# Other durations for float32r products in the list scheduler of a three-layer transformer kernel

## The chip, the cores and the metric

One core of a Trainium2 chip runs the whole program in one launch. The metric is the device time of that launch in microseconds (us); lower is better. TensorE (PE below) does the matrix products, VectorE (DVE), ScalarE (ACT) and GpSimd (POOL) work beside it, and SyncE (SP) issues the transfers (DMA).

## The reference, cut to what matters

T = 256 tokens, a model width of 1024, a feed-forward width of 2816, all in float32. Two layers of a first block are followed by one layer of a second block.

```python
for l in range(2):                                   # first block
    h = rmsnorm(x, norm_mix[l])
    aq, ak, av, iq, ik, iw, hq, hf, hi, hg, ga, gb = split(h @ w_in[l])
    y_attn = dsa_attention(rope(norm(aq)), rope(norm(ak)), av, rope(iq), rope(ik), iw)   # 8 heads, top-64 keys
    o = hgrn2_chunked(silu(hq), 1 - exp(log_f), hi, log_f)                               # 4 heads, decay per key
    merged = sigmoid(ga) * (y_attn @ w_proj_attn[l]) + sigmoid(gb) * (rmsnorm(o) * silu(hg) @ w_proj_hgrn[l])
    x = x + merged @ w_out[l]
    g, u = split(rmsnorm(x, norm_ffn[l]) @ w_ffn_in[l])
    x = x + (silu(g) * u) @ w_ffn_out[l]

sh1, sc1, g1, sh2, sc2, g2 = split(silu(c) @ ada_w + ada_b)      # second block
h = rms_norm(x, mix_pre_g) * (1 + sc1) + sh1
q, k, v, f_logit, conv_val, conv_gate = split(h @ w_in)
attn = fox_attention(q, k, v, log_sigmoid(f_logit + b_f))
u = silu(layer_norm(causal_depthwise_conv(conv_val * sigmoid(conv_gate))))
x = x + g1 * rms_norm(concat(attn, u) @ w_o, mix_post_g)
h = rms_norm(x, ffn_pre_g) * (1 + sc2) + sh2
x = x + g2 * rms_norm(swiglu_ffn(h), ffn_post_g)
```

## The kernel before, in words

Every matrix product with a weight is done as three products of rounded parts (the type float32r, F32R in the code): an activation is split into xH (rounded) and xL (the rest), a weight into wH and wL, and PE adds xH·wH, xL·wH and xH·wL in PSUM. A weight comes as a tile `raw` of 128x1024 (512 KB), ACT copies it to `wH` with rounding, and DVE subtracts to get `wL`. `raw` has four buffers, `wH` and `wL` six each. `split_into` (L887) does the same with an activation: ACT writes xH, DVE xL.

The helpers are named for the shape of their products: `pair_mm` has 256 columns (all tokens move past a weight tile), `token_mm`, `out_tm` (L908) and the `go` of `first_tm` (L1332) have 512 (weight columns move past a token half).

The program text writes operations in a readable order, and none of them is issued then. `Recorder.record` notes each with what it reads, writes and depends on, and a duration from `Recorder.cost` (L402). `Recorder.issue` then orders them on a model of the five engines, and only after that does `op.emit` (L400) issue each instruction, for which reason nearly all lines of the profile are L400. The order comes about so:

- the rank of an operation is its own duration and the longest chain of durations and hops behind it; with a bias this is its urgency, and PE's urgencies are rounded down to steps of QUANT = 5000 ns:

```python
op.rank = tail + op.cost + (LOAD_LATENCY if op.engine == "DMA" else 0.0)
op.urgency = op.rank + op.bias
if QUANT and op.engine == "PE":
    op.urgency = op.urgency // QUANT * QUANT
```

- the engine that can start first takes the most urgent of the operations that are ready by then and that find a buffer; among equals the one written first. Each engine runs its queue strictly in that order on the chip.
- the durations therefore act twice, in the ranks and in the model's clock, and through them on all engines.

Places of the program that the prediction speaks of:

- `modulated_tm` (L1524) norms and splits the input of the second block's feed-forward, and calls `first_tm`'s `go` for its first tile. For each token half t and each half of the width it scales (`z`, DVE), transposes four times (PE, into a bank `mm`), applies scale and shift (ACT or DVE, four operations of 128x128), and splits; then come the 24 products of that token half.
- `rstd_of` (L836) norms the convolution at L1680: PE sums squares into one bank of PSUM, DVE takes the reciprocal root in some nine small operations, `spread` (L853) transposes the result into the same bank, and DVE multiplies it in. The output projection `out_tm` (L1689) has four accumulators, side_1767 to side_1770, also banks of the group `side`.
- in a layer of the first block, `attend` (L927) runs a head of attention: logits on PE, the maximum on DVE, exponentials on ACT, the scaling of the probabilities on DVE, transposes and products on PE. The HGRN part (L1195 to L1243) climbs a ladder of levels: `blocks` (L1198) makes products of 32x32 from hk and hq, DVE copies them under a mask into `AC` (`copy_predicated`, L1215), and before each level scales hq and hk by the decay. After five levels the diagonal is copied out of `AC` (L1223).

Of the kernel before, what the change touches and what calls it, by code (L numbers as in the profile page):

```python
# [349 lines left out]
class Recorder:  # L350
# [52 lines left out]
    @staticmethod  # L403
    def cost(engine, method, args, kw, views, outs):
        n = int(np.prod((outs or views)[0].shape[1:]))
        psum = any(v.buf.space == "PSUM" for v in views)
        if engine == "DMA":
            v = (outs or views)[0]
            return max(v.shape[0] * n * 4 / 360.0, 640.0)
        if engine == "PE":  # L410
            if method == "transpose":
                return 109.0
            m = int(np.prod(args[1].shape[1:]))
            if args[1].dtype == F32R:
                return max(n * 0.4265, 109.0)
            cost = max(n, m) * 1.667 + 3.0

            return (cost + 81.0) / 4 if m == 32 else (cost + 53.0) / 2 if m == 64 and n > 64 else cost
        if engine == "S":
            ptr = sum(isinstance(kw.get(k), View) for k in ("bias", "scale"))  # L420
            return (51 if psum else 94) + 0.833 * n + 93 * ptr + (93 if "accum_out" in kw else 0)
        if method in ("max",):
            n = int(np.prod(args[1].shape[1:]))
        fast = not psum and method in ("tensor_copy", "tensor_scalar")
        ptr = sum(isinstance(a, View) for a in args[2:{"tensor_scalar": 4, "scalar_tensor_tensor": 3}.get(method, 2)])
        return (68 if method != "memset" else 7) + n / (1.92 if fast else 0.96) + 61 * ptr

    def issue(self):
# [49 lines left out]
        while len(order) < len(ops):  # L478
# [84 lines left out]
            if e == "PE":  # L563
                while t >= window + WINDOW:
                    warm = busy >= ACTIVE
                    busy, window, left = min(left, WINDOW) * rate, window + WINDOW, max(left - WINDOW, 0.0)
                cost, rate = (cost, 2.4) if warm else (max(2.0 * cost, 214.0), 1.2)
                rate = 0.0 if op.thin else rate
                inside = min(cost, window + WINDOW - t)
                busy, left = busy + inside * rate, cost - inside  # L570
# [1143 lines left out]
```

## Time and profile before

| | |
|---|---|
| median of 3 runs | 1130.52 us (1129.08 to 1131.61) |
| profiled execution, its own time | 1129.97 us |
| its span | 1128.2 us, mean granted clock 0.992 |
| PE busy | 1097.2 us (97%) |
| DVE busy | 857.5 us (76%) |
| ACT busy | 595.5 us (53%) |
| instructions | 22970 |

Instructions of PE are matmuls with their weight loads (PEld) beside them. Busy is the union of the times in which an engine had an instruction running. A wait is idle time with the event that ended it. The profile drops the numbers from the names of buffers; the listings of the order below keep them.

### The profile page before, as it was taken

Reading aid. Unit: us, or ns where it says so; the run is one execution under the profiler, and the core shown is the slowest. Engines: PE = TensorE matmul, PEld = TensorE weight load, DVE = VectorE, ACT = ScalarE, POOL = GpSimd, SP = SyncE. Lnnn points to the kernel's source line nnn. Section 1 sums busy time; section 2 is a strip of 40 time slices with the busy share of each in tenths; the row PEclk is TensorE's granted clock in tenths of the full one; section 3 lists DMA queues with packets and bytes.
Section 4 is the critical chain, followed back from the end, with each engine's and each line's share of the span. In section 5 each row is a group of like instructions: output and inputs, shape, how many; then the busy total and the mean of one; then the engine's idle time right before and its main releaser. Section 6 shows DMA issues by size and latency. Waiting matters only on the chain.

```text
span 1128.2 us, 22970 instructions
## 1 busy us (share of the span) xinstructions
PE 1097.2 (97%) x9388; PEld 1034.5 (92%) x9388; DVE 857.5 (76%) x1590; ACT 595.5 (53%) x905; POOL 7.2 (1%) x16
## 2 busy tenths in 40 slices
PE   6999999999999999999999999999899989999996
PEld 6988999999999999888999999999798578999995
DVE  7999976899966589998676998756879668554554
ACT  6744694644444467446744544444754665443442
POOL 1000000000000000000000000000000000000000
PEclk9999999999999999999999999999999999999998
DMA  7553534689956543643345899655457225556550
GB/s 263 186 180 111 197 123 169 207 314 337 335 190 217 189 154 117 210 146 133 132 172 196 288 346 334 218 201 195 145 176 201 95 76 184 175 186 219 189 169 37
DMA packets 59992, 217.47 MB, mean 193 GB/s; under 512 B 6872, under 2 KB 10096, under 8 KB 56816
## 3 DMA queue, kind: packets, MB, share of 16 engines
q1 hardware_dynamic: 59888, 216.02, 55.8%
q8 instruction: 73, 1.20, 0.4%
q14 instruction: 31, 0.25, 0.1%
HBM read 214.19 MB, written 1.63 MB: 191 GB/s over the span
## 4 chain that ended last, share of the span: by engine, by line
PE 89%; DVE 6%; ACT 3%; issue 1%; DMA 1%; SPq 0%; DVEq 0%; ACTq 0%
PE mm L400 60%; PE side L400 29%; ACT t L400 2%; DVE t L400 1%; DVE b L400 1%; DVE wL L400 1%; DMA raw<-in_W 1%; DVE small L400 1%; ACT wH L400 1%; ACT L604 0%; DVE c L400 0%; DVE xL L400 0%; DVE AC L400 0%; SPq L400 0%; DVE sc L400 0%
## 5 line engine op out<-in xcount | busy, mean ns | idle before, releaser
L400 ACT ACTIVATE wH<-raw 128x1024 fp32r<-128x1024 f32 (+1 forms) x390 | 369.0, 968 | 400.5 <-PE mm L400 221.1
L400 DVE TENSOR_TENSOR wL<-raw,wH 128x1024 fp32r<-128x1024 f32 (+1 forms) x390 | 425.6, 1112 | 151.3 <-ACT wH L400 149.4
L400 PE MATMUL mm<-xH,wH 128*128 128x256 f32 x1760 | 486.8, 279 | 9.2 <-ACT wH L400 9.2
L400 PE MATMUL mm<-xH,wL 128*128 128x256 f32 x1760 | 488.3, 280 | 0.8 <-DVE wL L400 0.8
L400 PE MATMUL mm<-xL,wH 128*128 128x256 f32 x1760 | 488.5, 279 | 0.5 <-DVE xL L400 0.5
L400 PEld LDWEIGHTS mm<-xH,wH 128*128 128x128 f32 x1760 | 330.6, 189 | 11.7 <-ACT wH L400 9.2
L400 PEld LDWEIGHTS mm<-xL,wH 128*128 128x128 f32 x1760 | 331.2, 189 | 3.4 <-issue 0.9
L400 PEld LDWEIGHTS mm<-xH,wL 128*128 128x128 f32 x1760 | 330.8, 189 | 3.5 <-DVE wL L400 1.7
L400 PE MATMUL side<-t,wH 128*128 128x256 f32 x704 | 127.6, 281 | 0.0
L400 PEld LDWEIGHTS side<-t,wH 128*128 128x128 f32 x704 | 108.2, 188 | 0.0
L400 PE MATMUL side<-t,wL 128*128 128x256 f32 x352 | 98.8, 281 | 0.0
L400 ACT ACTIVATE t<-t 128x512 f32<-128x512 f32 (+2 forms) x80 | 48.9, 620 | 39.8 <-DVE t L400 37.0
L400 PEld LDWEIGHTS side<-t,wL 128*128 128x128 f32 x352 | 66.2, 188 | 0.0
L400 DVE SCALAR_TENSOR_TENSOR E<-E,b 128x1024 f32<-128x1024 f32 x48 | 57.9, 1221 | 4.1 <-DMA E<-in_ada 3.9
L400 PE MATMUL side<-wH,t 128*128 128x512 f32 x176 | 57.3, 394 | 0.0
L400 DVE TENSOR_TENSOR t<-t,t 128x512 f32<-128x512 f32 (+2 forms) x78 | 53.1, 681 | 3.7 <-ACT t L400 2.9
L400 PE MATMUL mm<-b,wH 128*128 128x256 f32 x256 | 46.6, 283 | 0.0
L400 PE MATMUL side<-E,wH 128*128 128x256 f32 x256 | 46.4, 281 | 0.0
L400 DVE TENSOR_TENSOR t<-mm,rstd 128x512 f32<-128x512 f32 (+1 forms) x50 | 33.7, 678 | 14.4 <-PE mm L400 14.1
L400 PE MATMUL mm<-wH,xH 128*128 128x512 f32 x96 | 38.7, 412 | 1.9 <-ACT xH L400 1.9
L400 PEld LDWEIGHTS mm<-b,wH 128*128 128x128 f32 x256 | 39.9, 191 | 0.0
L400 PEld LDWEIGHTS side<-E,wH 128*128 128x128 f32 x256 | 39.3, 188 | 0.0
(205 smaller groups left out, 1198.7 us busy)
## 6 DMA issues: line engine op xcount, KB each, us to landing
raw<-in_W SPq DMA_DIRECT2D x348, 512.0 KB, 4.3
E<-in_ada SPq DMA_DIRECT2D x24, 1024.0 KB, 7.0
b<-c SPq DMA_DIRECT2D x16, 128.0 KB, 4.6
c<-in_xT SPq DMA_DIRECT2D x4, 256.0 KB, 5.1
raw<-in_W SPq DMA_DIRECT2D x4, 256.0 KB, 4.9
b<-in_c SPq DMA_DIRECT2D x2, 512.0 KB
out_y<-E SPq DMA_DIRECT2D x4, 256.0 KB, 2.0
c<-E SPq DMA_DIRECT2D x4, 143.0 KB, 3.4
```

What stands on the lines that cost most here:

```text
L400: op.emit = lambda: getattr(real, method)(*[get(a) for a in args], **{k: get(a) for k, a in kw.items()})
```

## The change

One expression in `Recorder.cost`: the duration that the scheduler takes for a product of float32r operands with n columns.

```diff
--- before.py
+++ after.py
@@ -412,7 +412,7 @@
                 return 109.0
             m = int(np.prod(args[1].shape[1:]))
             if args[1].dtype == F32R:
-                return max(n * 0.4265, 109.0)
+                return n / 2.4 + 8.0 if n <= 256 else n / 2.4 + 18.0
             cost = max(n, m) * 1.667 + 3.0
 
             return (cost + 81.0) / 4 if m == 32 else (cost + 53.0) / 2 if m == 64 and n > 64 else cost
```

For the two sizes that nearly all these products have, 256 columns go from 109.2 to 114.7 ns and 512 columns from 218.4 to 231.3 ns. The operations are the same ones, 8696 on PE, 1450 on DVE, 809 on ACT, 424 transfers; only their order on each engine differs, from the first microseconds to the last stretch.

PE at the entry of the second block's feed-forward, before (mm_1845 are the products of the first token half, mm_1861 those of the second; mm_1857 and mm_1860 are the banks into which the second half's input is transposed; the last number of a name tells one life of a buffer from the next):

```order
L400 MATMUL mm_1845_11731<-wL_1784_11565,xH_1815_11725 128x512
L400 MATMUL mm_1845_11731<-wH_1783_11555,xL_1816_11733 128x512
L400 MATMUL mm_1857_11771<-c_7_108,t512_1855_11762 128x128 x4
L400 MATMUL mm_1845_11731<-wH_1786_11632,xH_1815_11725 128x512
L400 MATMUL mm_1845_11731<-wL_1787_11649,xH_1815_11725 128x512
...
L400 MATMUL mm_1845_11731<-wH_1789_11668,xL_1816_11733 128x512
L400 MATMUL mm_1860_11806<-c_7_108,t512_1858_11776 128x128 x4
L400 MATMUL mm_1861_11814<-wH_1780_11542,xH_1815_11725 128x512
L400 MATMUL mm_1861_11814<-wL_1781_11552,xH_1815_11725 128x512
```

and now:

```order
L400 MATMUL mm_1845_11730<-wH_1783_11557,xL_1816_11732 128x512
L400 MATMUL mm_1845_11730<-wH_1786_11632,xH_1815_11724 128x512
L400 MATMUL mm_1845_11730<-wL_1787_11648,xH_1815_11724 128x512
...
L400 MATMUL mm_1845_11730<-wL_1790_11766,xH_1815_11724 128x512
L400 MATMUL mm_1845_11730<-wH_1789_11670,xL_1816_11732 128x512
L400 MATMUL mm_1857_11796<-c_7_108,t512_1855_11761 128x128 x4
L400 MATMUL mm_1860_11801<-c_7_108,t512_1858_11769 128x128 x4
L400 MATMUL mm_1861_11821<-wH_1780_11547,xH_1815_11724 128x512
L400 MATMUL mm_1861_11821<-wL_1781_11553,xH_1815_11724 128x512
```

The transposes into mm_1857 stood after 12 of the 24 products of mm_1845 and stand after all of them, next to those into mm_1860; mm_1861 follows directly in both.

PE at the norm of the convolution and the output projection of the second block, before (side_1736 is a bank of the last attention heads; side_1761 is the bank of the norm, with the sums 128x1 and the spread 128x128; side_1767 to side_1770 are the projection's accumulators):

```order
L400 MATMUL side_1767_11427<-wH_1677_11086,xL_1690_11313 128x512
L400 MATMUL side_1736_11437<-t512_1739_11424,b4_1674_11141 64x256
...
L400 MATMUL side_1864_11445<-c_7_108,c_1565_9229 128x128 x4
L400 MATMUL side_1761_11452<-c_10_75,b4_1760_11418 128x1 x2
L400 MATMUL side_1736_11437<-t512_1746_11448,b4_1674_11141 64x256
...
L400 MATMUL side_1768_11463<-wH_1670_11079,xH_1689_11303 128x512
...
L400 MATMUL side_1769_11480<-wH_1670_11079,xL_1690_11313 128x512
L400 MATMUL side_1761_11452<-c_7_108,small_1763_11461 128x128 x2
L400 MATMUL side_1769_11480<-wH_1677_11086,xH_1689_11303 128x512
...
L400 MATMUL side_1769_11480<-wH_1677_11086,xL_1690_11313 128x512
L400 MATMUL side_1770_11495<-wH_1670_11079,xH_1689_11303 128x512
```

and now:

```order
L400 MATMUL side_1736_11427<-t512_1746_11424,b4_1674_11135 64x128
...
L400 MATMUL side_1767_11446<-wH_1670_11076,xH_1689_11293 128x512
...
L400 MATMUL side_1767_11446<-wH_1677_11083,xL_1690_11303 128x512
L400 MATMUL side_1768_11457<-wH_1670_11076,xH_1689_11293 128x512
...
L400 MATMUL side_1769_11465<-wH_1670_11076,xH_1689_11293 128x512
L400 MATMUL side_1761_11467<-c_10_75,b4_1760_11443 128x1 x2
L400 MATMUL side_1769_11465<-wL_1671_11089,xH_1689_11293 128x512
...
L400 MATMUL side_1769_11465<-wH_1677_11083,xL_1690_11303 128x512
L400 MATMUL side_1761_11467<-c_7_108,small_1763_11474 128x128 x2
L400 MATMUL side_1770_11495<-wH_1670_11076,xH_1689_11293 128x512
```

The first products of side_1767 stood ahead of the last heads and stand behind them, three products of side_1769 stood between the spread and side_1770 and now none does; between sums and spread there were two products of the last head, six of side_1768 and three of side_1769, and there are five of side_1769.

DVE in the first layer, before (AC_304 takes the block products under a mask, once for each level; b4_115 and b4_268 are hq and hk; AT1_303 and b4_302 take the diagonal of AC; t512_209 and t512_216 are the probabilities of the first two heads):

```order
L400 COPY_PREDICATED AC_304_1237<-c_8_942,side_308_1244 128x256
...
L400 COPY_PREDICATED AC_304_1237<-c_8_942,side_309_1305 128x256
...
L400 TENSOR_TENSOR wL_300_1398<-raw_295_1089,wH_299_1233 128x1024
...
L400 ISA t512_209_1412,small_211_1413<-side_208_1341,pen1_114_1380 128x256
...
L400 TENSOR_SCALAR t512_209_1412<-t512_209_1412,small_214_1490 128x256
...
L400 TENSOR_SCALAR t512_216_1433<-t512_216_1433,small_221_1504 128x256
...
L400 TENSOR_TENSOR b4_115_493<-b4_115_493,t512_307_572 128x128x4
L400 TENSOR_TENSOR b4_268_1163<-b4_268_1163,t512_307_572 128x128x4
L400 COPY_PREDICATED AC_304_1237<-c_8_942,side_310_1535 128x256
```

and now:

```order
L400 COPY_PREDICATED AC_304_1226<-c_8_760,side_308_1219 128x256
...
L400 COPY_PREDICATED AC_304_1226<-c_8_760,side_309_1272 128x256
...
L400 TENSOR_TENSOR b4_115_418<-b4_115_418,t512_307_535 128x128x4
L400 TENSOR_TENSOR b4_268_1150<-b4_268_1150,t512_307_535 128x128x4
L400 COPY_PREDICATED AC_304_1226<-c_8_760,side_310_1322 128x256
...
L400 COPY_PREDICATED AC_304_1226<-c_8_760,side_311_1382 128x256
...
L400 COPY_PREDICATED AC_304_1226<-c_8_760,side_312_1451 128x256
L400 COPY AT1_303_91<-AC_304_1226 32x4x32 x4
L400 COPY b4_302_1021<-AC_304_1226 32x4x32 x2
...
L400 ISA t512_209_1553,small_211_1554<-side_208_1506,pen1_114_1346 128x256
...
L400 TENSOR_SCALAR t512_216_1562<-t512_216_1562,small_221_1643 128x256
```

Three of the five masked copies, with the scalings of hq and hk ahead of each and the copies of the diagonal, stood behind the first two heads and stand ahead of them.

## Rows read from the trace of the kernel before

**Rows 1.** The page, busy us, share of the span and instructions:

```profile
PE 1097.2 (97%) x9388; PEld 1034.5 (92%) x9388; DVE 857.5 (76%) x1590; ACT 595.5 (53%) x905; POOL 7.2 (1%) x16
```

**Rows 2.** Stretches: us, then busy us of PE, PEld, DVE, ACT, POOL, clock, DMA:

```profile
40.00:160.00 120.00, 119.75 (x1294) 108.64 (x1294) 110.57 (x288) 72.24 (x136) 0.53 (x1) 1.00 0.49 163
160.00:400.00 240.00, 239.77 (x2063) 239.57 (x2062) 181.47 (x232) 115.62 (x135) 0.52 (x1) 1.00 0.69 239
400.00:560.00 160.00, 158.63 (x1590) 145.05 (x1590) 141.73 (x343) 100.32 (x173) 0.00 (x0) 1.00 0.43 148
...
800.00:820.00 20.00, 16.26 (x123) 14.04 (x122) 17.17 (x37) 14.75 (x29) 0.00 (x0) 0.91 0.31 107
...
920.00:941.00 21.00, 16.79 (x72) 13.28 (x71) 18.25 (x61) 13.87 (x35) 0.00 (x0) 0.84 0.18 65
941.00:1118.60 177.60, 177.60 (x1256) 164.53 (x1254) 91.49 (x101) 76.75 (x93) 0.00 (x0) 1.00 0.51 173
1118.60:1128.20 9.60, 0.02 (x1) 0.00 (x0) 6.07 (x18) 2.02 (x4) 2.48 (x2) 0.60 0.29 109
```

**Rows 3.** Waits of PE: who waited for whom, us in total, times, longest:

```profile
PE mm L400 <- ACT wH L400: 9.2, 1, 9.2
PE mm L400 <- ACT xH L400: 4.4, 2, 2.5
```

**Rows 4.** Timeline of place 1: start us, duration, engine, operation, tiles, count:

```profile
937.52 0.60 PE L400 MATMUL mm<-c,t 128*128 128x128 f32 x4
...
937.88 0.48 PE L400 MATMUL mm<-wH,xH 128*128 128x512 f32 x1
...
938.16 1.51 ACT L400 ACTIVATE t<-mm,c,c 128x128 f32<-128x128 f32 x4 [2.82 <-PE mm L400]
...
939.70 0.63 ACT L400 ACTIVATE xH<-t 128x512 fp32r<-128x512 f32 x1
...
940.36 0.69 DVE L400 TENSOR_TENSOR xL<-t,xH 128x512 fp32r<-128x512 f32 x1
...
941.12 0.48 PE L400 MATMUL mm<-wH,xH 128*128 128x512 f32 x1
```

**Rows 5.** Stretches ahead of place 1, columns as in rows 2:

```profile
926.50:933.20 6.70, 2.55 (x13) 1.91 (x11) 6.24 (x28) 6.25 (x16) 0.00 (x0) 0.72 0.00 0
933.20:936.40 3.20, 3.14 (x8) 2.50 (x9) 2.95 (x12) 2.14 (x6) 0.00 (x0) 0.52 0.00 0
```

**Rows 6.** Timeline of place 2:

```profile
902.94 0.50 PE L400 MATMUL side<-c,b 128*128 128x1 f32 x4
...
903.48 0.16 DVE L400 TENSOR_SCALAR small<-side 128x2 f32<-128x2 f32 x1 [1.79 <-PE side L400]
...
905.68 0.16 DVE L400 SCALAR_TENSOR_TENSOR small<-small,small 128x2 f32<-128x2 f32 x1
...
906.36 0.38 PE L400 MATMUL side<-c,small 128*128 128x128 f32 x2
...
906.78 1.29 DVE L400 TENSOR_TENSOR b<-b,side 128x512 f32<-128x512 f32 x2 [0.94 <-PE side L400]
...
908.21 0.47 PE L400 MATMUL side<-wH,xH 128*128 128x512 f32 x1 [0.77 <-DVE b L400]
```

**Rows 7.** First layer: PE, then DVE timeline, one tile's row, and PE at the heads:

```profile
97.52 0.76 PE L400 MATMUL side<-b,b 128*32 128x32 f32 x64
98.21 0.39 PE L400 MATMUL mm<-xL,wH 128*128 128x256 f32 x1
...
98.51 1.28 DVE L400 TENSOR_TENSOR b<-b,b 128x512 f32<-128x512 f32 x2
99.70 0.45 DVE L400 COPY_PREDICATED AC<-c,side 128x256 f32<-128x256 uint8 x1
...
106.48 1.22 DVE L400 TENSOR_TENSOR wL<-raw,wH 128x1024 fp32r<-128x1024 f32 x1
...
L400 DVE COPY AT<-AC x8: 214/218/223, 138.1 to 507.0; 32x128 f32<-32x128 f32 x8
...
113.19 0.33 PE L400 MATMUL side<-c,t 128*128 128x128 f32 x1 [0.25 <-DVE t L400]
```

## The prediction

> **What bounds the kernel now.** Read first the busy shares [rows 1]: TensorE (PE) is busy for 1097.2 us of a span of 1128.2, so all that any order could gain is 31 us, most of it start and end. Then the table of stretches [rows 2]. The two big feed-forward stretches and the last one have no gap to speak of (239.77 of 240.00, 177.60 of 177.60): there the spacing of the products sets the time and any order gives the same. The attention stretch of the first layer has 0.25 us without PE, that of the second layer 1.37. The real holes are two changes of stage, 800 to 820 us (16.26 of 20.00) and 920 to 941 us (16.79 of 21.00, clock 0.84), and the end, 9.6 us in which PE does next to nothing. Then the waits of PE [rows 3]: the first weight costs 9.2 us, the split of an activation (xH) 4.4 in two waits; nothing else is as long. So the kernel is a stream of PE work whose order hides chains of VectorE (DVE) and ScalarE (ACT). The change alters no instruction and no duration on the chip. It can only lengthen or shorten gaps, and I ask at each place where the order moves whether the work that covers a chain is still there.
>
> The sum is made against the profiled execution, 1129.97 us; the median of the three runs shown, 1130.52, stands 0.55 above it. About 0.2%, 2.3 us, is what a measurement of this kernel can tell from no change.
>
> **What the new durations do.** A product of 256 columns was 109.2 ns to the scheduler and is now 114.7; one of 512 was 218.4 and is 231.3. In the trace twelve 512-column products and four transposes fill 937.88 to 941.12 us, the transposes 0.36 of it, which leaves (3.24 - 0.36) / 12 = 0.24 us a product [rows 4]. The new numbers are nearer. The Trainium skill (TensorE: Matmul & The Clock Gate, section "Wait — 56ns, not 53.3ns?") gives columns / 2.4 GHz plus about 2.5 ns for products back to back, 109 and 216 ns, which is the old table; the trace does not agree with it for these products. By that spacing the five products of place 2 would cover 0.1 us less and the sum would be 0.1 higher. Either way a truer duration does not buy a better order by itself: PE's urgencies are cut to steps of 5000 and ties go by program order, so a 5% change of the ranks shifts many ties, in both directions. The order shows three moves that touch a chain whose cover is thin.
>
> **Place 1, entry of the last feed-forward block, PE: +2.2 us.** Before, PE runs 12 products of the first token half, four transposes of the second half (mm_1857), 12 more products, the other four transposes (mm_1860), and then the second half's products (mm_1861). In the change all 24 products come first, then both groups of transposes, then mm_1861 at once. What must happen in between is in the trace [rows 4]: transposes at 937.52, four ACT operations from 938.16 for 1.51, the rounded copy xH from 939.70 for 0.63, ending 940.33, and DVE's xL from 940.36 for 0.69, ending 941.05. From the first transpose that is 2.81 us to xH and 3.53 to xL. Before, PE reaches mm_1861 at 941.12, 3.60 us after the transposes, and waits for nothing. In the change the cover is the eight transposes, 2 x 0.36 = 0.72. So PE waits 2.81 - 0.72 = 2.1 us, and the first product that reads xL, some 0.6 us later, waits 0.1 more. The second chain, from mm_1860, runs on DVE beside the first and is covered by the 12 products that follow (2.9 us). The wait is not given back: behind it PE has no gap until 1118.6 [rows 2]. Bounds: one instruction of the chain (0.69) less or more, 1.5 to 2.9.
>
> **Place 2, norm of the convolution in the second block, PE: +1.7 us.** Before, the first six output products (side_1767) stand between heads of the attention, ahead of the sums of the norm, and side_1768 and side_1769 follow the sums: three of them stand between the spread of the norm's scale and side_1770. In the change all of attention comes first, 13 products stand ahead of the sums, five between sums and spread, none between spread and side_1770. In the trace [rows 6] the sums start at 902.94, DVE's reciprocal root runs from 903.48 to about 905.84 with a foreign 0.42 us in it, so it is ready 2.4 to 2.9 us after the sums; cover in the change: the sums (about 0.25) and 5 x 0.24, 1.45 together. New wait about 1.0 (1.0 to 1.4). From the spread at 906.36 to side_1770 at 908.21 is 1.85 us, the bank being free only after DVE's two products of 1.29; before, three products lie in it and 0.77 us of wait is left. Without the three the wait is 0.77 + 0.7 = 1.47: +0.7. Together +1.7. Bounds: 0.8, if DVE, with attention done, gets through both chains a third faster (2.4 of 2.9 is such a case), and 2.5 if the upper ends fall together.
>
> **Place 3, attention of the first layer, DVE: +1.8 us.** DVE serves two things there: the ladder of HGRN block products (scaling of hq and hk per level, a masked copy into AC) and the heads of attention. Before, two masked copies come ahead of the first heads and three after them; in the change all five, with the copies of the diagonal, come ahead. From the product that starts AC to the scaling of the second head's probabilities DVE has 41 instructions before and 59 after. The extra ones: eight level products at 0.60 (two in 1.19 us, 98.51 to 99.70), three masked copies at 0.34 to 0.48, eight diagonal copies at 0.22, one weight remainder wL at 1.13 [rows 7]: 4.8 + 1.1 + 1.8 + 1.1 = 8.8 us; one scaling (0.69) and two maxima (0.28 to 0.4 each) have moved ahead of the stretch, and with them 1.1 or more goes: +7.7 at most. PE's own work in the same stretch grows too: 14 products of 512 columns (3.4 us), 112 small block products at 0.79 / 32 = 0.025 us (32 of them, recorded as 64, end at 98.21 and follow the product of 97.19) (2.8 us), eight small ones (0.9 at most, priced as a 256-column product), ten 256-column products fewer (-1.2): +5.9. PE already waits 0.25 us for the scaled probabilities at 113.19 [rows 7], so there is no slack in which the difference could vanish: 7.7 - 5.9 = +1.8. Lower end 0: DVE may be ahead when it gets there, since its HGRN work starts sooner. Upper end 3.6: the same move stands in the second layer, and would cost the same again.
>
> I cost the move in the second layer at nothing: before, PE lacks 1.37 us there [rows 2], and what is lost ahead of the heads can come back behind them, where the ladder's rest no longer stands in the way; without that cover it is the 1.8 of the upper end. DMA: 424 loads before and after; they keep their queue, and weights are loaded several tiles ahead, so with PE behind them by microseconds nothing waits for them that did not before. ACT's table loads stay 20. Start and tail are the same instructions in the same order: nothing.
>
> **Sum:** 2.2 + 1.7 + 1.8 = +5.7, 1129.97 + 5.7 = 1135.7 us.
>
> **Rivals.** (a) No change, about 1131: the waits only take the place of others. For it: PE is at 97%, and in the stretch around place 1 it already lacks 4.2 us [rows 2], so that a DVE queue that is ready sooner could pay for the new wait. Against: the wait of place 1 comes behind that gap, in a queue that runs in order. (b) Faster, about 1127: with truer products the scheduler fills gaps that it did not see. What can be had is the second layer's 1.37 us and perhaps a third of the 3.74 us of the stage change at 800: -2.6, with the three places costing nothing. Against: the rows say that the cover is gone at place 1, and -2.6 barely leaves the bound of what can be told. (c) Slower still, about 1139: PE's clock falls again at place 1. At 933.2 to 936.4 the granted clock is 0.52, so PE ran almost all of it at the lower of its two levels (1.2 of 2.4 GHz), and 8 products take 3.14 us where 8 x 0.24 = 1.9 would do [rows 5]; it follows a stretch in which PE was idle for more than half of the time (2.55 of 6.70). A second wait of 2.2 us soon after could bring this again, 3.14 - 1.9 = +1.2, and with the upper end of place 3 (another +1.8) the time is 1135.7 + 3.0 = 1138.7. Against: one wait of 2.2 us is shorter than the hole that precedes 933. The Trainium skill (TensorE: Matmul & The Clock Gate, section "HAM oscillation — how this bites in real kernels") describes it as waits on other engines that send PE back to its lower clock, so that the next burst starts slow; the row at 0.52 agrees, and whether this wait is long enough no run here shows yet.
>
> **How the numbers follow.** Forecast 0.50 (three places, with their bounds 1129.97 + 2.3 = 1132.3 to 1129.97 + 9.0 = 1139.0); (a) 0.20; (b) 0.15; (c) 0.15. Faster 0.15, same 0.20, slower 0.65. The range reaches down to 1129.0, taking in (a) and leaving out most of (b), and up to 1140.0, which takes in (c). The forecast's own range is 1132.3 to 1139.0.
>
> **What would show it.** In the changed profile: a PE wait of about 2 us, released by ACT's xH, behind two groups of four transposes some 2 us before the gap-free last stretch; a PE wait of about 1 us at the spread and 1.5 at side_1770; more PE idle time in 40 to 160 us, with DVE as the releaser. The prediction is wrong if these waits are there and the span is not longer (then a gap elsewhere has closed), or if PE reaches mm_1861 without a wait.

## The result and the profile after

The changed kernel takes 1143.74 us (median of 4 runs, 1141.48 to 1145.62) against 1130.74 us for the kernel before (4 runs, 1129.08 to 1131.61): a ratio of 1.0114, 95% interval 1.0096 to 1.0132, so 13.0 us slower. The forecast was 1135.7 us with a range up to 1140.0. The direction was right; the size was less than half of what came, and the time lies outside the range.

The profiled execution took 1141.48 us, its span 1139.7. The head of the page, to be held against [rows 1]:

```profile
span 1139.7 us, 22996 instructions
PE 1103.5 (97%) x9388; PEld 1034.7 (91%) x9388; DVE 855.5 (75%) x1590; ACT 594.8 (52%) x905; POOL 7.2 (1%) x16
```

The share of busy PE time is the same 97%: PE's busy time has grown by 6.3 us though the work is the same. Two things in the traces can do this. At the lower clock a 512-column product is recorded with 0.63 us instead of 0.39. And the records overlap: one of a 256-column product lasts 0.28 us and the next starts 0.11 behind it, so that a short stall leaves no gap. The shares don't show the loss. The table of stretches shows where, against [rows 2] (us, then busy PE, PEld, DVE, ACT, POOL, clock, DMA; the bounds are moved to the same work):

```profile
40.00:165.00 125.00, 122.80 (x1289) 108.89 (x1288) 112.61 (x294) 75.44 (x142) 0.52 (x1) 1.00 0.47 152
165.00:405.00 240.00, 239.84 (x2062) 239.63 (x2060) 177.91 (x226) 111.64 (x129) 0.53 (x1) 1.00 0.70 241
405.00:565.00 160.00, 158.47 (x1598) 143.72 (x1597) 144.41 (x347) 101.54 (x176) 0.00 (x0) 1.00 0.46 150
565.00:805.00 240.00, 238.78 (x2049) 238.34 (x2048) 177.30 (x233) 111.90 (x133) 0.00 (x0) 1.00 0.70 239
...
926.00:952.50 26.50, 20.37 (x85) 15.56 (x84) 21.37 (x68) 15.13 (x38) 0.00 (x0) 0.87 0.32 112
952.50:1130.20 177.70, 177.70 (x1249) 164.71 (x1247) 88.56 (x95) 75.86 (x91) 0.00 (x0) 0.99 0.52 167
```

The first layer's attention has 2.20 us without PE where it had 0.25, and takes 125 us instead of 120; the other 3 us are in PE's busy time. The feed-forward stretches are as they were, but for a hole of 1.2 us in the second one. The last stretch again has no gap, but it is no longer wholly at full clock. The waits of PE in the whole kernel, against [rows 3]:

```profile
PE mm L400 <- ACT wH L400: 9.8, 2, 9.3
PE mm L400 <- ACT xH L400: 6.6, 3, 2.5
PE mm L400 <- DVE t L400: 4.3, 4, 2.1
PE side L400 <- DVE b L400: 1.9, 2, 1.5
```

The third wait for xH is new, place 1; the wait for b at place 2 has grown from 0.77 us [rows 6] to 1.5.

To see where the time goes in a stream that hardly shows gaps, I laid both traces along PE's own work. Every product gets the median spacing that its kind has in the trace before (114 ns for 256 columns, 233 for 512); the start of a product less the sum of the spacings ahead of it in its kernel's order is what PE has lost up to there. The change loses, against before:

| PE work done | what lies up to there | loss so far, us |
|---|---|---|
| 60 us | up to the ladder of the first layer | 0.6 |
| 110 us | ladder and heads of the first layer | 5.2 |
| 380 us | first feed-forward | 5.2 |
| 440 us | projections of the second layer | 3.8 |
| 460 us | its ladder | 6.6 |
| 540 us | its heads and outputs | 4.2 |
| 680 us | second feed-forward, a late weight | 5.7 |
| 810 us | second block's input | 5.7 |
| 870 us | convolution and its norm (place 2) | 7.7 |
| 880 us | end of the output projection | 7.1 |
| 890 us | entry of the last feed-forward (place 1) | 12.0 |
| 1060 us | last product | 12.0 |

Three quarters of the loss stand at two of the forecast's three places, the first layer's ladder with its heads and place 1. Each curve is one execution; the median difference is 13.0.

Place 1, PE's timeline (the transposes, the waits and the first products behind each):

```profile
936.82 1.31 PE L400 MATMUL mm<-c,t 128*128 128x128 f32 x8 [2.09 <-DVE t L400]
...
940.35 0.79 PE L400 MATMUL mm<-wH,xH 128*128 128x512 f32 x1 [2.23 <-ACT xH L400]
...
948.56 1.03 PE L400 MATMUL mm<-c,t 128*128 128x128 f32 x8
...
951.41 0.50 PE L400 MATMUL mm<-wH,xH 128*128 128x512 f32 x1 [1.82 <-ACT xH L400]
```

and the clock around it, columns as above:

```profile
940.35:945.60 5.25, 5.25 (x12) 3.98 (x13) 5.08 (x18) 2.08 (x5) 0.00 (x0) 0.50 0.08 18
945.60:951.40 5.80, 3.99 (x21) 3.13 (x19) 4.19 (x10) 2.17 (x6) 0.00 (x0) 0.97 0.77 271
951.40:952.70 1.30, 1.29 (x5) 0.97 (x6) 1.30 (x3) 0.76 (x2) 0.00 (x0) 1.00 0.84 337
952.70:956.10 3.40, 3.40 (x11) 2.61 (x10) 1.83 (x4) 1.53 (x3) 0.00 (x0) 0.51 0.01 2
```

The two waits ahead of it were there before (2.34 and 1.87 us). The third, 1.82 us behind the eight transposes, is the one forecast at 2.1. What was not in the sum is the last row: 1.3 us after that wait the clock falls to the lower level a second time, for 3.4 us. The first stretch at the lower clock was there before too [rows 5], but shorter: 6 products of the kernel before, 12 here, have more than 0.38 us to the next. This makes some 1.1 of the 4.9 us that the table has for the place.

### The profile page after: what moved, and what is told of

Same layout as the page of the kernel before. It is cut to its first block, busy times and chain, and to the rows that moved or that the text cites. A ratio compares the mean times of both kernels' runs of the same rounds, so it can differ in the third digit from the quotient of the medians.

```text
span 1139.7 us, 22996 instructions
## 1 busy us (share of the span) xinstructions
PE 1103.5 (97%) x9388; PEld 1034.7 (91%) x9388; DVE 855.5 (75%) x1590; ACT 594.8 (52%) x905; POOL 7.2 (1%) x16
## 4 chain that ended last, share of the span: by engine, by line
PE 78%; DVE 11%; DMA 4%; ACT 4%; issue 2%; SPq 0%; DVEq 0%; ACTq 0%
PE mm L400 52%; PE side L400 26%; DMA raw<-in_W 4%; DVE wL L400 3%; DVE t L400 2%; ACT t L400 2%; ACT wH L400 1%; DVE b L400 1%; DVE small L400 1%; DVE sc L400 1%; DVE c L400 1%; ACT L604 1%; DVE E L400 1%; DVE xL L400 0%; DVE AC L400 0%
## 5 line engine op out<-in xcount | busy, mean ns | idle before, releaser
L400 PE MATMUL mm<-wL,xH 128*128 128x512 f32 x96 | 40.2, 419 | 0.0
```

The costliest lines, as they stand in the source:

```text
L400: op.emit = lambda: getattr(real, method)(*[get(a) for a in args], **{k: get(a) for k, a in kw.items()})
```

## The experiments

Two kinds of edit serve. A **bias** raises or lowers the urgency of one operation's instructions, so that little else moves. A **splice** makes both plans, with the old and the new durations, and issues one plan's instructions up to a landmark and then what is left in the other's order. Every splice keeps all instructions and dependences; the landmarks are a product in the middle of the first feed-forward (op 3100), one in the second (op 7000), and the first block product of the ladder (op 1055):

```diff
+        for which, cut in SPLICE:            # e3: ((new, 3100), (old, None))
+            for op in plans[which]:
+                if op.index == cut:
+                    break
+                if op.index not in seen:
+                    seen.add(op.index)
+                    out.append(op)
```

Times are medians in us; each ratio is against the kernel before on the same chip, with its 95% interval.

### e1 and e2: place 1 alone

```diff
+                        keep, R.bias = R.bias, R.bias + (-10000.0 if n == "ffn" and t == 1 else 0.0)
                         for i in range(4):
                             PE.transpose(ps[:, i * 128:i * 128 + 128], z[:, i * 128:i * 128 + 128], ident)
+                        R.bias = keep
```

e1 is the kernel before with this line, e2 the changed kernel with +10000.

> The kernel before with one place moved: the four transposes into mm_1857 stand after all 24 products of the first token half, as in the change (28 PE, 5 DVE and 3 ACT instructions change their position, nothing else). Theory W (the wait alone): PE waits about 1.8 us for the split of the second half, as measured in the changed kernel; the time is 1130.7 + 2 = 1132.7 us. Theory C (the wait brings the clock down again): beside the wait the products before or behind it run at the lower clock for some more us, as in the changed kernel's stretch 952 to 956 us; 1130.7 + 4 to 5 = 1135 us. Theory N (the place is not the cause, its wait only stands where earlier delays of the changed kernel put it): within 1 us of the kernel before.

Measured: 1134.59 against 1130.66, ratio 1.0034 (1.0022 to 1.0046), +3.9.

> The changed kernel with the four transposes into mm_1857 put ahead of the products again, and the other four soon behind them (51 PE and 7 DVE instructions change their position, all at this place). Theory W: 1143.7 - 2 = 1141.7 us. Theory C: 1143.7 - 5 = 1138.7 us, with no second fall of the clock behind the last attention. Theory N: 1143.7 us.

Measured: 1140.0, ratio 1.0086 (1.0073 to 1.01), 3.7 under the changed kernel's 1143.74. The runs of the two overlap (1137.51 to 1143.74 and 1141.48 to 1145.62), so this 3.7 is good to a microsecond or two.

Both ways the place is worth about 3.8 us. In e1 the wait alone is excluded (the interval starts at +2.5 us) and theory C met; e2 lies between the two. PE's waits in e1 from 920 to 965 us, below them stretches of the same kernel (columns as before), and PE's timeline at the third wait:

```profile
PE mm L400 <- ACT xH L400: 4.1, 2, 2.3
PE mm L400 <- DVE t L400: 2.3, 1, 2.3
```

```profile
932.90:939.20 6.30, 6.26 (x15) 4.67 (x16) 6.09 (x20) 2.12 (x5) 0.00 (x0) 0.50 0.25 82
939.20:944.30 5.10, 3.35 (x19) 2.61 (x17) 3.02 (x7) 2.12 (x6) 0.00 (x0) 1.00 0.82 275
944.30:945.90 1.60, 1.53 (x7) 1.16 (x8) 1.55 (x3) 0.81 (x3) 0.00 (x0) 1.00 0.30 123
945.90:949.20 3.30, 3.30 (x10) 2.51 (x9) 1.36 (x3) 1.36 (x3) 0.00 (x0) 0.52 0.00 0
```

```profile
941.52 1.04 PE L400 MATMUL mm<-c,t 128*128 128x128 f32 x8
944.37 0.50 PE L400 MATMUL mm<-wH,xH 128*128 128x512 f32 x1 [1.82 <-ACT xH L400]
...
945.90 0.50 PE L400 MATMUL mm<-wH,xL 128*128 128x512 f32 x1
...
949.54 0.39 PE L400 MATMUL mm<-wH,xL 128*128 128x512 f32 x1
```

One wait more of 1.8 us, and behind it a second stretch at the lower clock. Nine products start from 945.90 us on until 949.54; nine spacings of 0.233 would be 2.1 us instead of 3.64, so this stretch costs 1.5. In e2 it is gone with the wait: behind 920 us PE waits only twice, 2.1 and 2.2 us.

All profiles of this study agree, if the 512-column products with over 0.38 us to the next are counted behind these waits. The five kernels with the late transposes (the change, e1, e4, e8, e11) have a first run of 11 to 14 such products and a second one of 6 to 8. The other fifteen have no second run. Their first one has 6 to 12, and the kernel before (6) and e16 (12) have the same order there: how long the first stretch lasts goes with the execution, whether there is a second with the order.

At place 2 the order does not decide it. PE waits there for 0.43 and 1.47 us in the change, e2, e4, e8, e11 and e18 alike. In the profiles of e2 and e8 the clock falls right behind, against theory C's forecast for e2; in the other four it does not. The first row is of e2, the second of the changed kernel:

```profile
917.00:921.00 4.00, 4.00 (x12) 3.13 (x11) 2.57 (x5) 4.00 (x9) 0.00 (x0) 0.57 0.01 2
916.20:920.20 4.00, 4.00 (x19) 3.23 (x18) 2.52 (x5) 4.00 (x9) 0.00 (x0) 1.00 0.01 2
```

So place 2 costs more in some executions than in others.

### e3, e4 and e15: one stretch in the new order at a time

> The order of the change up to the middle of the first layer's feed-forward, the order of the kernel before from there on. Theory A (each stretch loses by itself, and the losses add): what the changed kernel had lost against before when its first feed-forward began, 5.2 us, stays: 1130.7 + 5.2 = 1135.9 us. Theory B (a delay early in the kernel is taken up by slack behind it, and the loss of the change is made later): 1130.7 to 1132 us.

Measured: 1136.57 against 1130.66, ratio 1.0056 (1.0044 to 1.0068), +5.9.

> The order of the kernel before up to the middle of the second layer's feed-forward, the order of the change from there on. Theory A: the losses of the second block in the changed kernel, 2.0 us around the norm of the convolution and 4.9 at the entry of the last feed-forward, less 0.6 between them: 1130.7 + 6.3 = 1137.0 us. Theory B: nearly the whole of 13 us, if the early losses would be made good: 1141 us or more.

Measured: 1137.03, ratio 1.0057 (1.0045 to 1.0069), +6.4.

> The order of the change from the middle of the first feed-forward to the middle of the second, the order of the kernel before elsewhere. Theory A (the losses of the stretches add): 11.9 - 5.9 - 6.3 leaves nothing, by the changed kernel's trace -1.0 in the layer: 1129.7 to 1130.7 us. Theory B (a layer's loss depends on the state in which it is entered): up to some microseconds either way.

Measured: 1129.87 against 1130.93, ratio 0.999 (0.9981 to 0.9999), -1.1.

The stretches nearly add: 5.9 + 6.4 - 1.1 = 11.2 of the 13.0 us. Theory A holds between layers as far as these runs go (e18 below departs from it): what is lost in one is not made good in the next. That the feed-forward of 240 us with hardly a gap between them is the reason is likely, not shown. Of the second block's 6.4, place 1 (e1) makes 3.9; the place of the rest is not settled by a run.

### e5, e13 and e14: what the first layer loses

```diff
+                        R.extra = -2000.0 if first else 0.0      # e5, added to the urgency
                         attend(h, logits, pens, rq8, av, y, "side")
+                        R.extra = 0.0
```

> The kernel before with one bias: in the first layer the heads of attention are 2000 less urgent, so that all five masked copies of the ladder stand ahead of the scaling of the second head (DVE positions 181 to 205, the scaling at 241; in the kernel before 181 to 265 and 215, in the change 182 to 208 and 236). The order outside this layer's middle stays. Theory L (the ladder ahead of the heads is what the first layer loses): 1130.7 + 2 to 5 = 1132.5 to 1135.5 us. Theory O (the loss of the first layer has other places: DVE and ACT work ahead of it, buffers, loads): within 1 us of the kernel before.

Measured: 1133.01 against 1130.62, ratio 1.0022 (1.0012 to 1.0032), +2.4.

> The order of the change only up to the first block product of the first layer's ladder (some 75 us), the order of the kernel before from there; at this point both orders have issued the same instructions but for 17 of PE and one of ACT. Theory L (the first layer loses in the ladder and the heads): 1130.7 to 1131.7 us, what the traces show at this point (0.6 to 1.0). Theory E (the loss is laid earlier, by DVE and ACT work that is late when the ladder begins): 1133 us or more.

Measured: 1133.99 against 1130.93, ratio 1.0024 (1.0015 to 1.0033), +3.1.

> The counterpart: the order of the kernel before up to the first block product, the order of the change from there to the middle of the first feed-forward, then before again. Theory L: 1130.7 + 4 to 5 = 1135 us. Theory E: 1132 us or less.

Measured: 1138.9, ratio 1.0064 (1.005 to 1.0078), +8.0.

The ladder ahead of the heads costs 2.4 by itself, as theory L has it and at its low end. But the two parts of the layer, 3.1 and 8.0, do not add to the 5.9 of both together (e3). Neither L nor E is right as put. Much of the difference is the clock, as e14 shows; PE's block products of the ladder, and below them stretches of that kernel:

```profile
96.01 0.63 PE L408 MATMUL side<-b,b 128*32 128x32 f32 x48 [1.57 <-DVE b L408]
97.97 0.44 PE L408 MATMUL side<-b,b 128*32 128x32 f32 x16 [0.60 <-DVE b L408]
```

```profile
75.00:90.00 15.00, 15.00 (x96) 13.27 (x95) 14.80 (x46) 4.96 (x6) 0.00 (x0) 1.00 0.72 231
90.00:97.00 7.00, 5.43 (x83) 3.89 (x81) 6.81 (x11) 5.16 (x7) 0.00 (x0) 0.97 0.24 81
97.00:105.00 8.00, 7.40 (x173) 4.98 (x173) 7.81 (x17) 1.23 (x2) 0.00 (x0) 0.60 0.44 131
```

The blocks wait for DVE's scalings of hq and hk (`b`), which stand in a queue that is full (DVE is busy for 14.80 of 15.00 and 6.81 of 7.00 us), and then the clock falls here too: 0.60 for 8 us. From 96.57 to 103.46 us PE does 7 products of 512 columns and 64 of the small ones; at 0.233 and 0.025 us these are 3.2 of the 6.9 us, the second wait is 0.6, and some 3 are left for the clock (an estimate from these rows). Without them e14 would cost about 5. In the changed kernel, and in e3, the clock stayed at 1.00 in this layer. The changed kernel's waits are smaller and lie in three places, the first ahead of the ladder at an evicted bank, the second inside the ladder; the third, of 0.27 us at 117.84, is that of the heads:

```profile
80.63 0.35 PE L400 MATMUL mm<-xH,wH 128*128 128x256 f32 x1 [0.78 <-DVE t L400]
...
107.55 0.83 PE L400 MATMUL side<-b,b 128*32 128x32 f32 x56 [0.45 <-DVE b L400]
```

They make 1.5 of the 5.2 us; the rest is in stalls too short to leave a gap, and no run separates them. The first of the three comes from the early part of the new order: e13 has it too, and longer,

```profile
80.63 0.35 PE L408 MATMUL mm<-xH,wH 128*128 128x256 f32 x1 [1.32 <-DVE t L408]
```

and in e13's profile nearly all of its loss, 1.7 us, arises there. The kernel before has no such wait. Why e13's median is higher, 3.1, stays open: five of its runs take 1132.5 to 1132.7 us, six 1134.0 to 1136.2, and the one profiled is of the first group.

### e6: the spread of the norm

```diff
+            R.bias = -2500.0
             r = rstd_of([flat(sq[:, i]) for i in two], 512)[2]
+            R.bias = 0.0
```

> The kernel before with the spread of the convolution's norm three products later, so that none stands between it and side_1770, as in the change; sums and spread have nine products between them instead of six. Theory S (cover of the spread): the wait at side_1770 grows from 0.77 to about 1.5 us, the time by 0.7, 1131.4 us. Rival: the bank is not what side_1770 waits for, or the wait is made good at the entry of the feed-forward, where PE waits anyway: 1130.7 us.

Measured: 1131.43 against 1130.62, ratio 1.0006 (0.9997 to 1.0014), +0.8. The size is that of theory S, but the interval reaches to no change: not settled by the time. In e6's own trace the wait at side_1770 is 1.47 us, as theory S has it. In the changed kernel's trace the two waits of place 2 stand as forecast, one at half of its size:

```profile
913.96 0.43 PE L400 MATMUL side<-c,small 128*128 128x128 f32 x2 [0.43 <-DVE small L400]
...
915.86 0.47 PE L400 MATMUL side<-wH,xH 128*128 128x512 f32 x1 [1.47 <-DVE b L400]
```

1.47 us at side_1770 is the value worked out; at the spread 0.43 came where 1.0 was expected, since DVE got through the reciprocal root in 1.6 us (912.30 to 913.90) with nothing foreign in it.

### e7 to e12: what of the new durations does it

```diff
-                return max(n * 0.4265, 109.0)
+                return n / 2.4 + 8.0 if n <= 256 else n * 0.4265                          # e7
+                return max(n * 0.4265, 109.0) if n <= 256 else n / 2.4 + 18.0             # e8
+                return max(n * 0.4265, 109.0) + (0.5 if n <= 256 else 1.0)                # e9
+                return max(n * 0.4265, 109.0) - (5.5 if n <= 256 else 12.9)               # e10
```

e11 keeps the old durations in the model's clock and takes the new ones for the ranks, e12 the other way round.

> The new duration for products of up to 256 columns alone (114.7 instead of 109.2 ns); 512 columns stay at 218.4. Its order keeps the early transposes at the entry of the last feed-forward. Theory P (the time is set by a few places whose cover is thin, so it goes with where the transposes stand): without the 3.9 us of that place, 1130 to 1139 us depending on the first layer. Theory D (a duration further from the chip gives a worse order, one nearer a better one): between the kernel before and the change, some 1137 us, as one half of the correction.

Measured: 1139.32 against 1130.62, ratio 1.0086 (1.0069 to 1.0103).

> The new duration for products of 512 columns alone (231.3 instead of 218.4 ns). Its order has the late transposes at the entry of the last feed-forward, as the change has. Theory P: at least 3.9 us over the kernel before, 1134.6 us or more. Theory D: some 1137 us, as the other half of the correction.

Measured: 1140.33, ratio 1.0085 (1.0072 to 1.0098).

> The durations of the kernel before with 0.5 ns more for 256 columns and 1.0 ns more for 512 (109.7 and 219.4), a change of a half per cent that says nothing of the chip. Its order differs from the kernel before in 5704 positions of PE. Theory T (the kernel before is a tuned point: its biases fit the order that its own durations give, and any other order loses some microseconds): 1133 to 1140 us. Theory D (what matters is how far the durations are from the chip): 1130.7 us within 1.

Measured: 1129.83 against 1130.55, ratio 0.9995 (0.9986 to 1.0003).

> The durations moved by the same amounts the other way (103.7 and 205.5 ns), away from the spacing in the trace. Theory T: some microseconds slower, about as the change or as either half of it, 1134 to 1144 us. Theory D in its one form (nearer is better) 1131 us or more, far more than the change only if distance counts; in its other form (the scheduler wants them too short) faster than 1130.7 us.

Measured: 1133.99, ratio 1.0029 (1.0019 to 1.0039).

> The new durations in the ranks alone; the model's clock counts the old ones. Its order has the late transposes and the ladder ahead of the heads, as the change. Theory R (the ranks move the ties, and through them the order): about the change, 1138 to 1144 us, at least 3.9 over the kernel before for the transposes. Theory K (the model's clock does it): within 2 us of the kernel before.

Measured: 1142.57, ratio 1.0104 (1.0091 to 1.0117).

> The new durations in the model's clock alone; the ranks use the old ones. Its order has the early transposes and the heads ahead of the ladder. Theory R: 1130 to 1134 us. Theory K: about the change, 1140 us or more.

Measured: 1138.78, ratio 1.0075 (1.0061 to 1.0089).

Theory P's bound for e8 is met; e7 lies just over the upper end of its own. e11 falls where theory R puts it, e12 between the two theories.

No single part carries the loss. Each half of the correction costs nearly as much as both; ranks alone cost 12.0 us, the clock alone 8.2. Theory D falls: the durations nearer to the chip give the slowest orders, those as far off on the other side cost 3.4. Theory T in its hard form falls too: e9 moves 5704 positions of PE and costs nothing. Theory R is right that the ranks bring the late transposes (e8 and e11 have them, e7 and e12 don't), but K's part is not nothing. Laid along PE's work as above, in their profiled executions, e12 loses 8.4 us in the first layer and 3.8 more by the end of the second (an execution of 1142.73 us, the longest of its six), e7 6.7 in the first, e11 6.6 in the first and some 5 at place 1. These are mostly the same stretches, but not always the same moves: e12 keeps the heads ahead of the ladder, and part of its loss is the clock, 0.51 from 41.0 to 44.5 us and from 88.8 to 92.3, where the changed kernel has 1.00.

### e16 to e18: parts put together

e16 is a splice of three pieces, before, the order of e10 from the middle of the first feed-forward to the middle of the second, and before. e17 adds +5000 on the norm's bias of e6. e18 is the order before up to the middle of the first feed-forward, then the order of the change with e2's bias.

> The kernel before, with the order that the durations moved the other way give (103.7 and 205.5 ns) from the middle of the first feed-forward to the middle of the second. In the trace of that whole kernel this stretch ran 2.6 us faster than before (3.0 us behind at its entry, 0.4 at its end). Theory A: 1130.7 - 2.6 = 1128.1 us, faster than the kernel before. Theory B: the gain there was only the taking up of the delay brought in; within 1 us of the kernel before.

Measured: 1127.91 against 1130.93, ratio 0.9968 (0.9956 to 0.9981), -3.0.

> The kernel of e16 with the spread of the convolution's norm ahead of all six products of side_1769 (a bias of 5000 on the norm). Theory S: the wait at side_1770, 0.77 us in the kernel before, is covered by three more products: 0.7 us under e16, 1127.2 us. Rival: what PE gains there it waits at the entry of the last feed-forward: 1127.9 us.

Measured: 1127.19 against 1130.67, ratio 0.9967 (0.9954 to 0.998), -3.5.

> The order of the kernel before through the first layer, the order of the change from the middle of its feed-forward, with the early transposes at the last feed-forward: the change without its two largest places. Theory A (losses add): 1130.9 - 1.1 (e15) + 6.4 (e4) - 3.9 (e1) = 1132.3 us. Theory B (the losses move to other places when two are taken away): 1135 us or more.

Measured: 1134.64 against 1130.67, ratio 1.0033 (1.002 to 1.0045), +4.0, runs from 1130.5 to 1136.1.

e16 beats both kernels, by the amount that its stretch showed in e10's trace: the gain was its own. Of what it consists is not shown. It is not idle time of PE: over the second layer's attention e16 has 1.64 us of gaps, the kernel before 1.37 [rows 2]:

```profile
400.00:560.00 160.00, 158.36 (x1616) 146.31 (x1615) 145.73 (x347) 101.34 (x176) 0.00 (x0) 1.00 0.46 151
```

Laid along PE's work, e10 and e16 both gain it between 493 and 506 us of the kernel before, while that climbs the second layer's ladder. e17's trace has no wait at side_1770, as theory S has it, but its time can't be told from e16's. e18 lies between its theories: the changed order without its two largest places still costs 4.0 us, not 1.6, so the account by stretches is good to some 2.5 us and no better.

## Why the prediction was wrong

**What bounds it** was right in that the kernel is a PE stream and gaps come where chains lose their cover. But PE's time is not only work and gaps: its busy time grew by 6.3 us, half of the loss, at the lower clock and in stalls that leave no gap. No term of the sum stood for that.

**"A truer duration does not buy a better order by itself"** was right, and was too mild: against the change, e9 and e10 show that it is not the distance from the chip that orders these times.

**Place 1, +2.2.** The wait was right (1.82 us against 2.1). The step that failed is the price of a wait as its own length. It measured +3.9 (e1), since the clock fell a second time behind it: 1.82 for the wait, some 0.3 for the products that start late right behind it (two of them have 0.34 us to the next instead of 0.233, and the first reader of xL waits a little), and 1.5 for the second stretch at the lower clock, 3.6 together. That was rival (c), put at a chance of 0.15 with the argument that "one wait of 2.2 us is shorter than the hole that precedes 933"; its price for the stretch, 1.2, was near. The wait comes some 10 us behind the hole; the row at 0.52 ahead of the place was the warning. The Trainium skill (TensorE: Matmul & The Clock Gate, section "HAM oscillation — how this bites in real kernels") describes a loop whose waits for transfers send PE back to its lower clock, so that the next burst starts slow. e1 and e2 agree in the direction: the wait put in brings the lower clock, and taken out, takes it away at this place. They go beyond it in the size: the waits described there are longer, and here 1.82 us for an ACT operation was enough, behind two of 2.3.

**Place 2, +1.7.** Mechanism and larger wait right (1.47 against 1.47); the smaller was 0.43 instead of 1.0, the term about 1.1. The trace lost 2.0 from 810 to 870 us of work; the two waits less the 0.77 of before are 0.43 + 1.47 - 0.77 = 1.1 of it. The clock behind them (e2 and e8 at 0.57) was in no term.

**Place 3, +1.8.** This is the largest miss: +5.9 for the first layer (e3). The step that failed is that "7.7 - 5.9 = +1.8", the difference of DVE's and PE's work between the ladder's start and the second head, stands for the whole layer. It lets DVE fall behind only at the end of the stretch and takes every instruction between as movable cover. But each level's block products need that level's two scalings, and DVE was 92% busy in the layer before the change (110.57 of 120.00 [rows 2]): in the changed kernel PE waits ahead of the ladder, in the ladder and at the heads. The ladder ahead of the heads alone, which is what the step priced, measured +2.4 (e5), close to it. The sum left out the rest of the layer's reordering, above all the order ahead of the ladder, which alone measured +3.1 (e13) with a wait at a bank that had none before. Which of the short stalls make up the rest stays open. The list of DVE's extra work is also one operation short: 41 + 20 - 3 is 58, and the count was 59.

**Second layer, nothing.** -1.1 (e15), at the edge of what can be told; the term was right. That the upper end of place 3 doubled it there was not.

**Start and loads, nothing.** They are not in the same order: PE's order differs from its 20th instruction on, and 81 of the 424 transfers changed their position. The trace lost 0.6 us up to the ladder. In the changed kernel's second feed-forward ACT waited 2.7 us for a `raw` tile and PE 1.1 for its wL, a loss of 1.5 in that profile. Whether other executions have it was not tried.

**The range.** Its upper end took in rival (c), so it gave the clock one more fall, at place 1. What was missing is the loss outside the three chains: a reordering of 6672 of 8696 PE positions has places that were not looked at.

## What to carry to other kernels

Where a schedule comes from a model with ties and tuned biases, treat a correction of its durations as a new draw of the order, measure it, and keep the better stretch of each: here the splice of e16 gained 0.3% where the truer table cost 1.1%. When an order moves, price an uncovered wait by its length and then look at the clock rows ahead of it: a wait of 1.8 us cost 3.9. Where a second engine is over 90% busy in a stretch, don't price its reordering by one chain; its queue can turn other moves into small stalls of the first engine. And don't look for those in the gaps alone: a stall shorter than the overlap of two records shows only as busy time.

## What the runs showed of the hardware

A PE wait of 1.82 us, coming some 10 us after two of 2.3, was followed by 3.3 us at a granted clock of 0.52 (e1, and so in all five kernels with this wait). In the first layer two waits of 1.57 and 0.60 us within 3 us were followed by 8 us at 0.60 (e14), while three waits of 0.78, 0.45 and 0.27 us spread over 37 us left it at 1.00 (the changed kernel). Two waits of 0.43 and 1.47 us within 3 us were followed by 4 us at 0.57 in two profiles (e2, e8) and left the clock at 1.00 in four (the change, e4, e11, e18): the same waits with either outcome.

Some orders also spread more from run to run: the kernel before lies within 3.2 us over 21 runs (1128.96 to 1132.11), the changed one spans 4.1 us in 4, e7 7.7 us in 6. It does not go with the loss alone: e10 spans 1.3 us in 8 runs and e8 1.1 in 4.
